# RMSNorm with SiLU on one core: stores move from SyncE's queue to ScalarE's, loads are issued one block earlier

## The chip, the core and the metric

The kernel runs on one core of a Trainium2 chip. Five engines work side by side, each on its own list of instructions, in order: TensorE (PE), VectorE (DVE), ScalarE (ACT), GpSimd (POOL) and SyncE (SP). An instruction waits on semaphores for what it needs, and everything behind it on the same engine waits with it. Transfers between HBM and the on-chip memory are issued by an engine's queue (here SyncE's and ScalarE's) and carried out by 16 DMA engines, which report each finished transfer on a semaphore.

The metric is the time of the whole kernel on the device, in microseconds (us). A profile records one execution; its span runs from the first to the last instruction, and the time of the same execution is a little longer than its span.

## The reference

```python
x = np.random.randn(8, 1024, 2048).astype(np.float32)
gamma = np.random.randn(2048).astype(np.float32)
eps = np.float32(1e-5)

def reference(x, gamma, eps):
    rms = np.sqrt(np.mean(x ** 2, axis=-1, keepdims=True) + eps)
    out = gamma * x / rms
    return (out * (1 / (1 + np.exp(-out)))).astype(np.float32)
```

Each of 8192 rows of 2048 numbers is divided by its root mean square, multiplied by gamma, and passed through SiLU. 64 MiB are read and 64 MiB written.

## The kernel before

The 8192 rows are cut into 16 blocks of 512 rows. A block is one tile `xt` of 128 partitions by 4 rows of 2048 floats (32 KiB in each partition, 4096 KB in all), and it is loaded by one transfer and stored by one transfer. The pool holds six such tiles (`BUFS` = 6, line 33). A load needs a tile that is free, that is, one whose earlier block has been stored.

Before the loop, the row of gamma is fetched by ScalarE's queue (line 93) into one of these six tiles, five blocks are loaded by SyncE's queue (lines 95 and 96, line 51), and TensorE spreads gamma to all partitions by a matrix product with a column of ones (line 99); VectorE copies the result into the tile `g` (line 100).

Then, for each block b, `work(b)` does this:

- The sums of squares of its four rows: two on ScalarE (line 79, Square with accumulation), two on VectorE (line 82).
- `rsqrt` (lines 61 to 72) on VectorE: 15 instructions on 128 x 4 numbers, which give 1/rms by a bit trick and four Newton steps, without ScalarE.
- For each of the four rows, VectorE multiplies by `g` in place (line 87), then ScalarE applies Silu in place with 1/rms as its scale (line 88).
- SyncE stores the tile (line 89). The store waits for the last Silu of the block.

After `work(b)`, SyncE gets the load of block b + LEAD, with LEAD = 5 (lines 103 and 104). It takes the tile of block b - 1, so it waits until the store of block b - 1 has landed. (Block 5 takes the tile in which the row of gamma stood.)

The order is as written: the kernel runs under `manual_schedule`, so each engine gets its instructions in program order, and only semaphores between engines are added. SyncE's list is therefore: loads 0 to 4, store 0, load 5, store 1, load 6, and so on to store 10, load 15, and then stores 11 to 15. A wait of one entry holds all that stand behind it. All these transfers go through one DMA queue. A transfer's semaphore is one of a set of eight that are used again in turn, so a transfer may also have to wait until an older one with the same semaphore has landed.

Of the kernel before, what the change touches and what calls it, by code (L numbers as in the profile page):

```python
# [1 line left out]

# [4 lines left out]

ACT = mybir.ActivationFunctionType
ALU = mybir.AluOpType


@with_exitstack
def kernel(
    ctx: ExitStack,
    tc: tile.TileContext,
    x: bass.AP,
    gamma: bass.AP,
    eps: bass.AP,
    out: bass.AP,
):  # L20

    nc = tc.nc
    P = nc.NUM_PARTITIONS
    f32, i32 = mybir.dt.float32, mybir.dt.int32
    x2 = x.flatten_outer_dims()
    o2 = out.flatten_outer_dims()  # L30
    n, d = x2.shape
    J = 4
    BUFS, LEAD = 6, 5
    nblk = n // (P * J)
    xb = x2.rearrange("(b p j) d -> b p (j d)", p=P, j=J)
    ob = o2.rearrange("(b p j) d -> b p (j d)", p=P, j=J)

    singles = ctx.enter_context(tc.tile_pool(name="singles", bufs=1))
    pool = ctx.enter_context(tc.tile_pool(name="pool", bufs=BUFS))
    small = ctx.enter_context(tc.tile_pool(name="small", bufs=2))  # L40
    psum = ctx.enter_context(tc.tile_pool(name="psum", bufs=1, space=bass.MemoryType.PSUM))

    g = singles.tile([P, d], f32)
    ones = singles.tile([1, P], f32)
    junk_a = psum.tile([P, d], f32, name="junk_a")
    junk_v = psum.tile([P, d], f32, name="junk_v")
    blocks = {}

    def load(b):
        xt = pool.tile([P, J * d], f32, name="xt")  # L50
        nc.sync.dma_start(out=xt, in_=xb[b])
        blocks[b] = xt

    def row(b, j):
        return blocks[b][:, j * d:(j + 1) * d]

    def rsqrt(ss):


        var = small.tile([P, J], f32, name="var")  # L60
        nc.vector.tensor_scalar(out=var, in0=ss, scalar1=1.0 / d, scalar2=float(eps),  # L61
                                op0=ALU.mult, op1=ALU.add)
        y = small.tile([P, J], f32, name="y")
        t = small.tile([P, J], f32, name="t")
        nc.vector.tensor_single_scalar(out=t.bitcast(i32), in_=var.bitcast(i32), scalar=1,  # L65
                                       op=ALU.logical_shift_right)
        nc.vector.tensor_scalar(out=y.bitcast(i32), in0=t.bitcast(i32), scalar1=-1, scalar2=0x5F375A00,  # L67
                                op0=ALU.mult, op1=ALU.add)
        for _ in range(4):
            nc.vector.scalar_tensor_tensor(out=t, in0=y, scalar=-0.5, in1=y, op0=ALU.mult, op1=ALU.mult)  # L70
            nc.vector.tensor_mul(out=t, in0=t, in1=var)  # L71
            nc.vector.scalar_tensor_tensor(out=y, in0=t, scalar=1.5, in1=y, op0=ALU.add, op1=ALU.mult)  # L72
        return y

    def work(b):
        ss = small.tile([P, J], f32, name="ss")
        for j in (0, 2, 1, 3):
            if j < J // 2:
                nc.scalar.activation(out=junk_a, in_=row(b, j), func=ACT.Square,  # L79
                                     accum_out=ss[:, j:j + 1])  # L80
            else:
                nc.vector.tensor_tensor_reduce(  # L82
                    out=junk_v, in0=row(b, j), in1=row(b, j), scale=1.0, scalar=0.0,
                    op0=ALU.mult, op1=ALU.add, accum_out=ss[:, j:j + 1])
        rstd = rsqrt(ss)
        for j in range(J):
            nc.vector.tensor_mul(out=row(b, j), in0=row(b, j), in1=g)  # L87
            nc.scalar.activation(out=row(b, j), in_=row(b, j), func=ACT.Silu, scale=rstd[:, j:j + 1])  # L88
        nc.sync.dma_start(out=ob[b], in_=blocks.pop(b))

    with tc.manual_schedule():
        grow = pool.tile([P, J * d], f32, name="xt")
        nc.scalar.dma_start(out=grow[0:1, 0:d],
                            in_=bass.AP(tensor=gamma.tensor, offset=gamma.offset, ap=[[d, 1], gamma.ap[0]]))
        for b in range(min(LEAD, BUFS - 1)):
            load(b)
        nc.vector.memset(ones, 1.0)  # L97
        for c in range(0, d, 512):
            nc.tensor.matmul(junk_v[:, c:c + 512], ones, grow[0:1, c:c + 512], start=True, stop=True)  # L99
        nc.vector.tensor_copy(out=g, in_=junk_v)  # L100
        for b in range(nblk):
            work(b)
            if b + LEAD < nblk:
                load(b + LEAD)


# [1 line left out]
_INS = ['x', 'gamma', 'eps']  # L108
_OUTS = [((8, 1024, 2048), 'float32')]

_NUMBERS = {'eps': 9.999999747378752e-06}


# [26 lines left out]
```

## Time and profile before

| | |
|---|---|
| Median of three runs | 321.74 us (321.55 to 322.38) |
| The profiled execution | 322.38 us, its span 320.6 us |
| Moved | 67.12 MB read, 67.11 MB written, 419 GB/s over the span |
| Loads, issue to landing | median 30.1 us, shortest 12.3 us |
| Stores, issue to landing | median 38.5 us (30.0 to 46.1) |
| Silu, one row of a block on ScalarE | 2.00 us, 64 of them |
| Multiplication by g, one row on VectorE | 2.28 us, 64 of them |
| Square on VectorE / on ScalarE, one row | 2.30 us / 1.87 us, 32 of each |
| ScalarE idle until line 87 of VectorE | 87.1 us in 62 waits |
| VectorE idle until line 79 of ScalarE | 20.0 us in 15 waits |

The page of a profile gives each engine's busy time and its share of the span; groups of instructions are named by line, engine and operation, `out<-in`. `xt<-in_x_dram` is a load and `out_dram<-xt` a store. "Idle before" is the time in which an engine stood still just before such an instruction, with what ended the wait. In a timeline each row gives the start in us from the span's start, the duration, the engine, the line and the operation; `SPq` and `ACTq` are the queues of SyncE and ScalarE, where an entry is the issuing of a transfer and not the transfer itself. `L121` and `L135` are lines around the kernel, at its start and its end.

### The profile page before, as it was taken

To read this page: it belongs to the slowest core of one execution; us is meant where nothing else is said; L and a number is where in the kernel's file an instruction comes from. 1 tells how busy PE (TensorE), PEld (TensorE's weight loads), DVE (VectorE), ACT (ScalarE), POOL (GpSimd) and SP (SyncE) were. 2 spreads that over 40 slices of the span, in tenths; PEclk is the share of its full clock that TensorE was granted. 3 is DMA by queue.
4 is the path that set the end of the run, shared out by engine and by line. 5 is a ranking of instruction groups with operands and counts; after the bars stand their busy time and mean duration, and the time that the engine had idled before them with its cause. 6 is when DMAs were issued, how large, how long until landed. Compare 5 with 4: busy or idle time off the path is not lost.

```text
span 320.6 us, 656 instructions
## 1 busy us (share of the span) xinstructions
PE 7.2 (2%) x8; PEld 2.5 (1%) x8; DVE 256.7 (80%) x370; ACT 193.1 (60%) x130; POOL 0.2 (0%) x4
## 2 busy tenths in 40 slices
PE   6200000000000000000000000000000000000000
PEld 2000000000000000000000000000000000000000
DVE  0699797989989797979899797979798997979000
ACT  1339486684939395775939393957759393948100
POOL 0000000000000000000000000000000000000000
DMA  8999999999999999999999999999999999999991
GB/s 328 446 405 458 421 429 392 430 417 442 425 425 446 409 450 430 421 437 418 437 446 409 442 429 425 437 429 433 433 414 442 442 421 442 421 433 450 409 446 82
DMA packets 4614, 134.26 MB, mean 419 GB/s; under 512 B 513, under 2 KB 513, under 8 KB 513
## 3 DMA queue, kind: packets, MB, share of 16 engines
q1 hardware_dynamic: 4608, 134.22, 97.8%
q14 instruction: 4, 0.03, 0.0%
q10 hardware_dynamic: 2, 0.01, 0.0%
HBM read 67.12 MB, written 67.11 MB: 419 GB/s over the span
## 4 chain that ended last, share of the span: by engine, by line
DVE 38%; issue 13%; ACT 8%; DVEq 1%
DVE xt L87 30%; ACT junk_a L79 7%; DVE t L70 2%; DVE t L71 2%; DVE y L72 2%; ACT xt L88 1%; DVEq L135 1%; DVE var L61 1%; DVE y L67 1%; DVE t L65 1%
## 5 line engine op out<-in xcount | busy, mean ns | idle before, releaser
L88 ACT ACTIVATE xt<-xt,y 128x2048 f32<-128x2048 f32 x64 | 128.1, 2002 | 92.5 <-DVE xt L87 87.1
L87 DVE TENSOR_TENSOR xt<-xt,g 128x2048 f32<-128x2048 f32 x64 | 142.2, 2283 | 0.0
L82 DVE CUSTOM_DVE_ANT_0 junk_v<-xt 128x2048 f32<-128x2048 f32 x32 | 73.5, 2296 | 1.7 <-DMA xt<-in_x_dram 1.1
L79 ACT ACTIVATE junk_a<-xt 128x2048 f32<-128x2048 f32 x32 | 59.9, 1872 | 11.0 <-DMA xt<-in_x_dram 10.5
L61 DVE TENSOR_SCALAR var<-ss 128x4 f32<-128x4 f32 x16 | 2.7, 170 | 20.1 <-ACT junk_a L79 20.0
L70 DVE SCALAR_TENSOR_TENSOR t<-y 128x4 f32<-128x4 f32 x64 | 10.4, 162 | 2.2
L72 DVE SCALAR_TENSOR_TENSOR y<-t,y 128x4 f32<-128x4 f32 x64 | 10.4, 162 | 2.2
L71 DVE TENSOR_TENSOR t<-t,var 128x4 f32<-128x4 f32 x64 | 10.4, 162 | 2.2
L100 DVE COPY g<-junk_v 128x2048 f32<-128x2048 f32 x1 | 2.3, 2292 | 8.7 <-PE junk_v L99 8.7
L99 PE MATMUL junk_v<-xt,ones 1*128 1x512 f32 x8 | 7.2, 1069 | 2.5 <-DMA xt<-in_gamma_dram 2.5
L79 ACT ACTIVATION_READ_ACCUMULATOR junk_a<-xt 128x1 f32 x32 | 6.0, 186 | 0.0
L82 DVE DVE_READ_ACCUMULATOR2_ANT ss<- 128x1 f32 x32 | 4.5, 140 | 0.0
L67 DVE TENSOR_SCALAR y<-t 128x4 int32<-128x4 int32 x16 | 2.7, 170 | 0.5
L65 DVE TENSOR_SCALAR t<-var 128x4 int32<-128x4 int32 x16 | 2.7, 170 | 0.5
L99 PEld LDWEIGHTS junk_v<-xt,ones 1*128 1x128 f32 x8 | 2.5, 322 | 5.6 <-issue 5.6
L79 ACT ACT_TABLE_LOAD x1 | 1.3, 1283 | 1.3 <-PEq L121 1.3
L88 ACT ACT_TABLE_LOAD x1 | 1.3, 1283 | 0.0
L97 DVE MEMSET ones<- 1x128 f32 x1 | 0.2, 165 | 0.8 <-PEq L121 0.8
L121 POOL MEMSET const-bfloat16-1.0<- 128x1 bf16 x1 | 0.1, 103 | 0.0
L121 POOL MEMSET const-uint8-127<- 128x1 uint8 x1 | 0.1, 103 | 0.0
L121 POOL MEMSET const-float32-1.0<- 128x1 f32 x1 | 0.1, 100 | 0.0
L121 POOL MEMSET const-float32-0.0<- 128x1 f32 x1 | 0.1, 99 | 0.2 <-issue 0.2
## 6 DMA issues: line engine op xcount, KB each, us to landing
xt<-in_x_dram SPq DMA_DIRECT2D x16, 4096.0 KB, 30.1
out_dram<-xt SPq DMA_DIRECT2D x16, 4096.0 KB, 38.5
xt<-in_gamma_dram ACTq DMA_DIRECT2D x1, 8.0 KB
```

Source lines behind the costliest of these rows:

```text
L61: nc.vector.tensor_scalar(out=var, in0=ss, scalar1=1.0 / d, scalar2=float(eps), op0=ALU.mult, op1=ALU.add)
L65: nc.vector.tensor_single_scalar(out=t.bitcast(i32), in_=var.bitcast(i32), scalar=1, op=ALU.logical_shift_right)
L67: nc.vector.tensor_scalar(out=y.bitcast(i32), in0=t.bitcast(i32), scalar1=-1, scalar2=0x5F375A00, op0=ALU.mult, op1=ALU.add)
L70: nc.vector.scalar_tensor_tensor(out=t, in0=y, scalar=-0.5, in1=y, op0=ALU.mult, op1=ALU.mult)
L71: nc.vector.tensor_mul(out=t, in0=t, in1=var)
L72: nc.vector.scalar_tensor_tensor(out=y, in0=t, scalar=1.5, in1=y, op0=ALU.add, op1=ALU.mult)
L79: nc.scalar.activation(out=junk_a, in_=row(b, j), func=ACT.Square, accum_out=ss[:, j:j + 1])
L82: nc.vector.tensor_tensor_reduce(out=junk_v, in0=row(b, j), in1=row(b, j), scale=1.0, scalar=0.0, op0=ALU.mult, op1=ALU.add, accum_out=ss[ ...
L87: nc.vector.tensor_mul(out=row(b, j), in0=row(b, j), in1=g)
L88: nc.scalar.activation(out=row(b, j), in_=row(b, j), func=ACT.Silu, scale=rstd[:, j:j + 1])
L99: nc.tensor.matmul(junk_v[:, c:c + 512], ones, grow[0:1, c:c + 512], start=True, stop=True)
L135: with _tile.TileContext(nc) as tc:
```

## The change

The look-ahead grows from five blocks to six, one more load stands before the loop, and stores are issued by ScalarE's queue.

```diff
-    BUFS, LEAD = 6, 5
+    BUFS, LEAD = 6, 6
...
         for j in range(J):
             nc.vector.tensor_mul(out=row(b, j), in0=row(b, j), in1=g)
             nc.scalar.activation(out=row(b, j), in_=row(b, j), func=ACT.Silu, scale=rstd[:, j:j + 1])
-        nc.sync.dma_start(out=ob[b], in_=blocks.pop(b))
+        nc.scalar.dma_start(out=ob[b], in_=blocks.pop(b))
...
         for b in range(min(LEAD, BUFS - 1)):
             load(b)
...
         nc.vector.tensor_copy(out=g, in_=junk_v)
+        load(BUFS - 1)
         for b in range(nblk):
             work(b)
             if b + LEAD < nblk:
                 load(b + LEAD)
```

SyncE's list is now the 16 loads alone. Load 5 waits for the tile in which the row of gamma stood; load b + 6 takes the tile of block b and waits until store b has landed. ScalarE's list gets 16 stores, each between the last Silu of its block and the Squares of the next. The arithmetic, the tiles and the number and size of the transfers are the same.

## The prediction

> **What bounds the kernel now.** I read the busy shares and DMA queues of the page first, then SyncE's waits, then the timeline of one block and the last stretch.
>
> ```profile
> PE 7.2 (2%) x8; PEld 2.5 (1%) x8; DVE 256.7 (80%) x370; ACT 193.1 (60%) x130; POOL 0.2 (0%) x4
> ...
> q1 hardware_dynamic: 4608, 134.22, 97.8%
> ```
>
> One queue carries every load and store and keeps the 16 DMA engines busy for 97.8% of the span: the kernel is bound by transfers, 32 of 4096 KB. SyncE's own waits say how these are paced:
>
> ```profile
> SPq L51 <- DMA out_dram<-xt: 178.8, 10, 20.1
> SPq L89 <- ACT xt L88: 95.0, 9, 18.8
> SPq L135 <- DMA out_dram<-xt: 21.4, 1, 21.4
> ```
>
> Loads wait for an older store to land (the buffer), in all 178.8 us; 21.4 us pass between the last issue and the last landing. The timeline of SyncE dates the landings, since each of these loads goes out as a store lands:
>
> ```profile
> 62.91 0.33 SPq L51 DMA_DIRECT2D xt<-in_x_dram  x1
> ...
> 82.61 0.33 SPq L51 DMA_DIRECT2D xt<-in_x_dram  x1
> ...
> 102.69 0.33 SPq L51 DMA_DIRECT2D xt<-in_x_dram  x1
> 103.07 0.42 SPq L89 DMA_DIRECT2D out_dram<-xt  x1
> ...
> 242.42 0.33 SPq L51 DMA_DIRECT2D xt<-in_x_dram  x1
> ```
>
> Store 0 (blocks count from 0) landed at 62.91, store 9 at 242.42: nine pairs of a load and a store in 179.5 us, 19.95 us a pair. Between load 0 (its first reader starts at 13.02) and 62.91 lie five transfers, 9.98 each. From 242.42 to the end (the last issue starts at 297.9, its copies land 21.4 later, near 319.7) lie eight, six of them stores: 9.66 each. The stretches of the end:
>
> ```profile
> 298.00:313.00 15.00, 0.00 (x0) 0.00 (x0) 0.00 (x0) 0.00 (x0) 0.00 (x0) 1.00 0.99 426
> 313.00:321.00 8.00, 0.00 (x0) 0.00 (x0) 0.00 (x0) 0.00 (x0) 0.00 (x0) 1.00 0.16 70
> ```
>
> The last two columns are the DMA share and GB/s. All engines are done computing before 298, the transfers run full until 313, and then only 0.16 of the DMA engines still work: some lag some 6 us behind the others, and the slowest sets the end. Compute is second in line, close behind. One block seen on ScalarE and VectorE:
>
> ```profile
> 29.77 2.00 ACT L88 ACTIVATE xt<-xt,y 128x2048 f32<-128x2048 f32 x1 [0.20 <-DVE xt L87]
> 31.68 1.86 ACT L79 ACTIVATE junk_a<-xt 128x2048 f32<-128x2048 f32 x1
> 31.80 0.35 SPq L89 DMA_DIRECT2D out_dram<-xt  x1
> ...
> 35.73 0.17 DVE L61 TENSOR_SCALAR var<-ss 128x4 f32<-128x4 f32 x1 [1.34 <-ACT junk_a L79]
> ```
>
> The last Silu of a block, the two Squares of the next, then VectorE's small steps (which wait 1.34 for the Squares) and its four multiplications, then the last Silu again: a closed chain, 17.73 us a block. It never starves after block 0, so it ends at 31.77 + 15 x 17.73 = 297.8. A block takes 17.73 us of compute and 19.95 of transfers; compute stays ahead because the first five loads run ahead of any store.
>
> **The change, part by part.**
>
> *Removed from SyncE:* 16 stores, 0.33 to 0.42 us each, and with them the order "load k+5 behind store k". That store had to wait for the block's last Silu (95.0 us in all). Worth nothing by itself: the queue was full behind it.
>
> *Load 5 ahead of block 0, the rest one ahead* (LEAD 6). Load 5 now waits only for the gamma row's buffer, which the matmuls free near 9.7, instead of going out at 32.24. The first five loads fill the queue until about 52, so nothing moves sooner: 0 us. Load k+6 waits for store k to land, the same store that frees its buffer now. Sixteen loads, 4096 KB each, stay on SyncE; nothing but loads stands behind a waiting load there.
>
> *Sixteen stores on ScalarE's queue.* Each stands between a block's last Silu and the next block's Squares, and must wait for that Silu to end. Now the Square starts 0.09 before the Silu's end (31.68 against 31.77). Afterwards: 0.09 lost, 0.03 to release (31.77 to 31.80), the issue, and 0.04 to the next instruction (the gamma issue ends at 1.24, the table load after it starts at 1.28). The issue is 0.33 to 0.42 on SyncE and 0.51 for the gamma row on ScalarE. So 0.49 to 0.67, I take 0.58. It lies on the closed chain, 15 times before the last block is done: 7.4 to 10.1, I take 8.7, and compute could end at 306.5 at best. Squares, VectorE's small steps and multiplications all queue behind. The program's order also gives stores 4 to 12 a wait for an older transfer, because they reuse its semaphore: store 5 for load 6, store 11 for load 12, the others for stores three to five blocks older. Those stores landed a block or more before; load 6 lands near 113 against 123 needed, load 12 near 232.5 against 233.2, and the Square behind that store needs load 12 anyway. I cost these waits at 0; if loads slip further, ScalarE stands still with the load, which it would do one instruction later.
>
> *Two rings in place of one.* This decides. From store 0 on, loads and stores no longer take turns of 4 MB in the order of one queue; both wait at the DMA engines all the time. The trace never has two full queues, so the share is bounded: loads first (then nothing starves), stores first (loads fall back until stores run out of computed blocks), and I take one for one, which is what the single queue gives in steady state. The pace of a pair is bounded by 19.32 (twice 9.66, if the stalls of the lagging engines disappear) and something above 19.95. I take 19.95, the row with the same mixture.
>
> Then: store 0 goes out at 31.8, and its bytes move about 1 us later, as load 0's do. At 33.0 the loads done are 1 + (33.0 - 13.0) / 9.98 = 3.0, so 13.0 remain. Now they go one for one with stores: 33.0 + 13.0 x 19.95 = 292.4 for load 15. In the old order it went out at 242.42 behind load 14 and store 10 and landed near 242.4 + 3 x 9.8 = 272. ScalarE would reach its Squares at 280.0 + 8.7 = 288.7: the load is late, load 14 (272.4 against 270.4 needed) slightly so. From landing to the last Silu block 0 shows 13.0 to 31.77, 18.8 us. So block 15 is computed at 292.4 + 18.8 = 311.2. At 292.4 13 stores are done; stores 13 and 14 run until 292.4 + 2 x 9.66 = 311.7, and store 15 follows: 321.4 (from a standstill, by load 0's 12.3, it would be 323.5). I take 321.6. Span 320.6 - 319.7 = 0.9 behind it: 322.5, against 320.6 now, +1.9 us. The profiled execution took 322.38, 0.64 more than the median of the three; the same difference on the median gives 323.6, and with the pace possibly between the two ends I say **323.4 us** (+0.5%).
>
> The Trainium skill speaks against the change: "DMA: Bandwidth & Descriptors", section "Issuing engines are not separate DMA queues", says that transfers started by several engines run on the same 16 DMA engines, interleave, and save no more than the time to issue. No row here shows two full queues. By this rule alone the sum would be the transfers' 319.7 again at best, so no gain, and the cost on ScalarE on top.
>
> **The rivals.**
>
> 1. *The rings cover each other's stalls* (faster). The 6 us that some engines lag may come from changes between loads and stores in one queue; with a second queue such an engine has other work. For it: the 0.16 row, and 9.66 for stores alone against 9.98 mixed. Against: a mixture now occurs at every packet. Price: pace 19.32, load 15 at 33.0 + 13.0 x 19.32 = 284.2, in time; compute sets the end: 306.5, and the last store alone 9.66 to 12.3, I take 11.1: 317.6, span 318.5, -2.1: 319.6 us. It ends on the other side; it decides from a pace under about 19.7.
>
> 2. *Stores get more than half, or mixing slows the engines.* If stores run out of computed blocks, load 15 lands with one store more done, one transfer later: +10 us, 333.4. Each 1% on the pace costs 2.6 us at load 15. For it: the mixture costs 0.3 us a transfer now at its few borders. Against: nothing in the trace shows a slow stretch of mixed work (full shares throughout).
>
> 3. *Loads come first, or nothing moves.* Load 15 lands as early as now, compute ends at 306.5, the slowest DMA engine still ends near 319.7: 321.7 us.
>
> **How the numbers follow.** Forecast 0.42 (322 to 325), rival 1 0.30 (317.5 to 320.5), rival 2 0.18 (326 to 334), rival 3 0.10. Differences under 0.3% (about 1 us, 320.8 to 322.7) can't be told from no change with this kernel. Faster: rival 1 and a little of rival 3, 0.32. Same: the rest of rival 3 and the lower edge of the forecast, 0.17. Slower: 0.51. Range 317.8 to 331: it holds rival 1 down to its short last store and rival 2 up to three quarters of its price.
>
> **What would show it.** Right: 20 us a load and 20 us a store side by side, load 15 landing near 292, ScalarE and VectorE waiting for loads from block 13 on, a ScalarE issue of some 0.4 us and a period of 18.3 us before that, VectorE's wait before line 61 near 1.9. Wrong: load 15 before 288 with the end still set by compute (rival 1), a long VectorE wait for loads in the middle (rival 2), ScalarE held at a store by an older transfer, or an issue that takes ScalarE a microsecond.

## The result, and the profile after

The changed kernel takes 319.48 us (median of 4, 319.35 to 319.61) against 321.64 us (median of 4, 321.17 to 322.38): a ratio of 0.9931, 95% interval 0.9911 to 0.995. It is 0.7% faster where 0.5% slower was forecast; the first rival had 319.6. The profiled execution has a span of 317.6 us, 3.0 less than before; it was the shortest of its four, and that of the kernel before the longest of its four, so this is more than the 2.2 us between the medians.

Busy shares and DMA queues, from the page of the changed kernel:

```profile
PE 7.2 (2%) x8; PEld 2.5 (1%) x8; DVE 256.8 (81%) x370; ACT 194.8 (61%) x130; POOL 0.2 (0%) x4
...
q1 hardware_dynamic: 2304, 67.11, 49.5%
q10 hardware_dynamic: 2306, 67.12, 49.0%
```

Two rings (a ring is the list of packets that one queue has waiting at the DMA engines) now carry half the bytes each. Together they are busy for 98.5% of 317.6, or 312.8 us of an average DMA engine; the one ring had 97.8% of 320.6, or 313.5 (312.7 and 313.7 by the packet records, without the rounding of the shares). So the mean work of an engine fell by only some 1.0 us while the end came 3.0 us earlier: what changed is mostly how far the slowest engine lies behind the mean.

One block border, from the timeline of the changed kernel (start, duration, engine, line, operation):

```profile
29.62 2.00 ACT L88 ACTIVATE xt<-xt,y 128x2048 f32<-128x2048 f32 x1 [0.20 <-DVE xt L87]
31.65 0.38 ACTq L89 DMA_DIRECT2D out_dram<-xt  x1
...
32.07 1.88 ACT L79 ACTIVATE junk_a<-xt 128x2048 f32<-128x2048 f32 x1 [0.45 <-ACT xt L88]
...
36.14 0.17 DVE L61 TENSOR_SCALAR var<-ss 128x4 f32<-128x4 f32 x1 [1.90 <-ACT junk_a L79]
```

The Square starts 0.45 us after the Silu's end, and VectorE waits 1.90 for it instead of 1.34. The issues of later stores lie 18.26 us apart: 0.53 us more a block.

Who waited for whom on the engines, and on SyncE, in the changed kernel:

```profile
DVE var L61 <- ACT junk_a L79: 27.8, 15, 1.9
ACT junk_a L79 <- DMA xt<-in_x_dram: 10.3, 1, 10.3
ACT junk_a L79 <- ACT xt L88: 6.3, 15, 0.5
...
DVE junk_v L82 <- DMA xt<-in_x_dram: 0.8, 1, 0.8
```

```profile
SPq L51 <- DMA out_dram<-xt: 217.3, 10, 45.7
SPq L136 <- DMA out_dram<-xt: 51.3, 3, 29.0
SPq L136 <- DMA xt<-in_x_dram: 33.9, 1, 33.9
```

Compute waits for a load once, at the first block, as before. Nothing starves. The last load is issued at 231.1 (the last start of line 51). After it SyncE stands at the end of the program (line 136) and waits for what is still under way: first for a store that lands at 251.4, then 33.9 for the last load, which lands at 285.3, then for the thirteenth store at 287.7 and 29.0 more for the last one, at 316.7. Load 15 is 7 us earlier than the forecast's 292.4 and close to the rival's 284.2.

The end of the changed kernel, the timeline first and then the same stretches as before (the last two columns are DMA share and GB/s):

```profile
303.57 2.00 ACT L88 ACTIVATE xt<-xt,y 128x2048 f32<-128x2048 f32 x1 [0.20 <-DVE xt L87]
305.61 0.34 ACTq L89 DMA_DIRECT2D out_dram<-xt  x1
```

```profile
298.00:313.00 15.00, 0.00 (x0) 0.00 (x0) 5.54 (x3) 6.98 (x4) 0.00 (x0) 1.00 0.84 360
313.00:321.00 8.00, 0.00 (x0) 0.00 (x0) 0.00 (x0) 0.00 (x0) 0.00 (x0) 1.00 0.31 131
```

Compute ends at 305.6 instead of 297.8. Before it ends most DMA engines have run out of work (a share of 0.54 from 303 to 308), and then all carry the last store, which lands at 316.7.

The packet records of the trace show where the lag went. Nearly every 32 KB packet takes 1.213 us. The excess over that, summed over all 16 engines (packets over by 0.05 us or more):

| Kernel | first 60 us | after 60 us |
|---|---|---|
| before | 25.3 us | 18.0 us |
| changed | 23.5 us | 2.2 us |

Both pay at the start and once more when the first store begins. After that the kernel before loses some 2 us (summed over the engines) in every 20, mostly in the last load packets ahead of a store, most of it on a few of the sixteen engines: five end 3 to 6 us later than most of the others. In the changed kernel this is nearly gone.

### The profile page after: what moved, and what is told of

Same layout as the page of the kernel before. It is cut to its first block, busy times and chain, and to the rows that moved or that the text cites. A ratio compares the mean times of both kernels' runs of the same rounds, so it can differ in the third digit from the quotient of the medians.

```text
span 317.6 us, 637 instructions
## 1 busy us (share of the span) xinstructions
PE 7.2 (2%) x8; PEld 2.5 (1%) x8; DVE 256.8 (81%) x370; ACT 194.8 (61%) x130; POOL 0.2 (0%) x4
## 3 DMA queue, kind: packets, MB, share of 16 engines
q1 hardware_dynamic: 2304, 67.11, 49.5%
## 4 chain that ended last, share of the span: by engine, by line
DVE 58%; ACT 27%; issue 4%; DMA 4%; ACTq 2%; DVEq 1%
DVE xt L87 44%; ACT junk_a L79 17%; ACT xt L88 10%; DMA xt<-in_x_dram 4%; DVE t L70 3%; DVE t L71 3%; DVE y L72 3%; ACTq L89 2%; DVE junk_v L82 1%; DVE t L65 1%; DVE var L61 1%; DVE y L67 1%; DVEq L136 1%; DVE ss L82 0%; DVEq L61 0%
## 5 line engine op out<-in xcount | busy, mean ns | idle before, releaser
L79 ACT ACTIVATE junk_a<-xt 128x2048 f32<-128x2048 f32 x32 | 60.2, 1881 | 17.1 <-DMA xt<-in_x_dram 10.3
L71 DVE TENSOR_TENSOR t<-t,var 128x4 f32<-128x4 f32 x64 | 10.3, 161 | 2.2
```

## The experiments

Several theories were to be told apart on the gain (A: two rings take the stalls out; B: the longer look-ahead; E: the stalls come from contention with compute; G or H: what about a second ring does it), and on what sets the end now (C: compute and the last store; D: the slowest DMA engine; D': that engine is slow because it also fetches instructions; F: it is slow for an unknown reason). A border is a place in a ring where a load is followed by a store.

**The queue alone** (`queue_only`)

```diff
     BUFS, LEAD = 6, 5
...
-        nc.sync.dma_start(out=ob[b], in_=blocks.pop(b))
+        nc.scalar.dma_start(out=ob[b], in_=blocks.pop(b))
```

> The stores on ScalarE's queue, LEAD left at 5, no extra load ahead of the loop. Theory A (two rings take the stalls out of the load-to-store borders; the look-ahead does nothing, since SyncE's list is loads alone either way): the same as the changed kernel, 319.5 us, within 0.3%; span near 317.6, last issue of a store near 305.6. Theory B (the gain is the earlier load 5 and the longer look-ahead): back to 321 to 322 us.

Measured 319.59 us, ratio 0.9947 (0.9928 to 0.9966): theory A. The look-ahead and the early load 5 are worth nothing measurable.

**The look-ahead alone** (`lead_only`)

```diff
-    BUFS, LEAD = 6, 5
+    BUFS, LEAD = 6, 6
...
         nc.sync.dma_start(out=ob[b], in_=blocks.pop(b))
...
+        load(BUFS - 1)
```

> LEAD 6 and load 5 ahead of the loop, the stores left on SyncE's queue. Theory A: no gain; worse, because in SyncE's one list load b+6 now waits for the landing of store b ahead of the issue of store b+1, so that the ring runs empty once a pair; from store 0 on some 1 to 2 us lost a pair, 12 pairs, 335 to 350 us. Theory B: 319 to 320 us.

Measured 354.55 us, ratio 1.1039 (1.1013 to 1.1066): the direction of theory A, and worse than its range. SyncE's queue in the timeline:

```profile
31.80 0.34 SPq L89 DMA_DIRECT2D out_dram<-xt  x1
73.54 0.33 SPq L51 DMA_DIRECT2D xt<-in_x_dram  x1
73.96 0.38 SPq L89 DMA_DIRECT2D out_dram<-xt  x1
96.48 0.33 SPq L51 DMA_DIRECT2D xt<-in_x_dram  x1
96.90 0.38 SPq L89 DMA_DIRECT2D out_dram<-xt  x1
```

Store 1 was ready at 49.5 and goes out at 73.96, behind a load that waits for store 0 to land. Each such landing finds the ring empty, and a pair takes 22.9 us (73.54 to 96.48) instead of 19.95. Idle engines are only half of the loss. The page of this run has the mean engine busy for 93.3% of its span of 353.8 us:

```profile
q1 hardware_dynamic: 4608, 134.22, 93.3%
```

That is 330 us of work against 313.7 in the kernel before, for the same bytes: half of the 33 us by which the span grew are slow packets. By the packet records a pair has some 28 us of excess over the 16 engines: some 11 in the first packets after the empty ring (0.7 us an engine) and some 15.5 where the load turns to the store (1.0 us an engine). The two halves of the change belong together: a look-ahead as long as the pool is only affordable when stores don't stand behind the loads.

**The store behind the next block's Squares** (`late_store`)

```diff
+    def finish(b):
+        nc.scalar.dma_start(out=ob[b], in_=blocks.pop(b))
+        if b + LEAD < nblk:
+            load(b + LEAD)
...
+        if b > 0:
+            finish(b - 1)
         rstd = rsqrt(ss)
...
-        nc.scalar.dma_start(out=ob[b], in_=blocks.pop(b))
...
-            if b + LEAD < nblk:
-                load(b + LEAD)
+        finish(nblk - 1)
```

> The changed kernel with each store issued on ScalarE after the two Squares of the next block (the last one after the last Silu), where ScalarE waits for VectorE anyway. Both theories of the end: the 0.53 us a block on ScalarE go, the period falls from 18.26 to 17.73 and the last store is issued near 298 instead of 305.6. Theory C (compute and the last store set the end): 2 to 4 us faster than the changed kernel, 315.5 to 317.5 us. Theory D (the slowest DMA engine, never idle, sets the end at 316.3 of the span): the same as the changed kernel, 319 to 319.8 us.

Measured 319.08 us, ratio 0.9929 (0.9913 to 0.9946), 0.4 us less than the changed kernel (and 0.5 less than `queue_only`, measured beside it): theory D. The 0.53 us a block did go from ScalarE (VectorE waits 1.34 again), but compute now waits 7.8 us for loads on VectorE and the last store leaves at 301.3. Its last stretches:

```profile
308.00:313.00 5.00, 0.00 (x0) 0.00 (x0) 0.00 (x0) 0.00 (x0) 0.00 (x0) 1.00 0.97 419
313.00:318.00 5.00, 0.00 (x0) 0.00 (x0) 0.00 (x0) 0.00 (x0) 0.00 (x0) 1.00 0.03 13
```

A share of 0.03 over 5 us of 16 engines is 2.4 us of one engine: fifteen are done by 313.7, and one alone works until 316.0. In the changed kernel the packets of the last store, which waits for compute, end at 316.2 to 316.4, and one engine that never stands idle before that store carries its last packet until 316.3. Two limits lie on top of each other, and removing one shows the other.

**The last store in four pieces** (`split_last`)

```diff
+            if b == nblk - 1:
+                nc.scalar.dma_start(out=ob[b][:, j * d:(j + 1) * d], in_=row(b, j))
+        if b < nblk - 1:
             nc.scalar.dma_start(out=ob[b], in_=blocks.pop(b))
```

> The changed kernel with the last block stored in four pieces of one row each, each issued behind its Silu. Theory C: the transfer left behind the last Silu shrinks from 4096 to 1024 KB, the DMA engines' idle time near 302 goes: 1.5 to 3 us faster than the changed kernel, 316.5 to 318 us. Theory D: within 0.3% of the changed kernel, 319 to 319.8 us.

Measured 319.27 us, ratio 0.9937 (0.992 to 0.9954): 0.2 us under the changed kernel where theory C had 1.5 to 3: theory D again.

**A copy on one ring, and on two** (`copy_one_ring`, `copy_two_rings`): the kernel before and the changed kernel without their compute.

> The kernel before with all of work(b) left out but the store: x is copied to the output by the same 32 transfers in the same order on SyncE's one ring. Theory A (the border from a load to a store in one ring costs some engines 0.2 to 0.8 us, whatever the compute engines do): the same slow packets near the last load packet before each store, the slowest engine some 4 to 6 us behind the fast ones, 318 to 322 us. Theory E (the stalls come from compute engines reading and writing the tiles beside the transfers): the stalls go, 314 to 316 us.

> The changed kernel with all of work(b) left out but the store: the same copy, stores on ScalarE's ring. Theory A: no slow packets after the first store's start, all engines end within 1 us of each other, 313.5 to 316 us; 4 to 6 us less than the copy on one ring. Theory E: the same as the copy on one ring.

Measured 320.41 us (median of 10, 319.12 to 321.58) on one ring and 316.83 us (median of 4, 316.58 to 318.96) on two; against the kernel before on the same chip 0.997 (0.9954 to 0.9986) and 0.9854 (0.9818 to 0.989). The rings alone are worth 3.6 us by the medians, with no compute beside them: theory A holds in the main, and E falls as the only cause. The excess after 60 us is 9.0 us on one ring and 2.1 us on two. Three things limit this. The gain is a little under the 4 to 6 us expected. The profiled executions took 319.12 us on one ring and 318.96 us on two, so the traces show the difference in the slow packets and not in their spans: on two rings one engine still ended 2.2 us behind the others. And on one ring the slow packets begin only at 120 us and add up to half of the 18.0 us in the kernel before; whether compute adds the other half, or single executions differ by as much, isn't shown.

**Twice the borders in one ring** (`halves_in_turn`, and `halves_in_pairs` to compare with)

```diff
-        nc.sync.dma_start(out=xt, in_=xb[b])
...
+        return [(xt[:, c:c + H], xb[b][:, c:c + H]) for c in (0, H)]
...
-            work(b)
-            if b + LEAD < nblk:
-                load(b + LEAD)
+            s = work(b)
+            l = load(b + LEAD) if b + LEAD < nblk else []
+            issue([p for two in zip(s, l) for p in two] if l else s)
```

> The kernel before with each transfer cut into two of 2048 KB (two rows of each partition), and SyncE's list in the loop: half a store, half a load, half a store, half a load. Twice as many borders from load to store in one ring. Theory A: the lag of the slowest engine doubles, 4 to 8 us over the next kernel's time. Otherwise: the same time as the next.

> The same halves, listed as two halves of the store, then two halves of the load: as many borders as the kernel before. All theories: 320 to 324 us, if the smaller transfers and their more frequent semaphores cost nothing; it is what the kernel before it is compared with.

Measured 322.15 us in turn and 323.30 us in pairs (ratios 1.0013, 1.0001 to 1.0025, and 1.0043, 1.0024 to 1.0062). The kernel with twice as many borders is not slower but 0.4% faster, and both lose the same after 60 us (8.6 and 8.4 us, in packets half as long). So the loss is not a fixed price for each border: that part of theory A fell.

**Two rings, each with both directions** (`copy_mixed_rings`)

```diff
+    def ring(b):
+        return nc.scalar if b % 2 else nc.sync
...
-        nc.sync.dma_start(out=xt, in_=xb[b])
+        ring(b).dma_start(out=xt, in_=xb[b])
...
-        nc.sync.dma_start(out=ob[b], in_=blocks.pop(b))
+        ring(b).dma_start(out=ob[b], in_=blocks.pop(b))
```

> The copy without compute (all of work(b) left out but the store), both loads and stores of even blocks on SyncE's ring and of odd blocks on ScalarE's: two rings, but each with borders from loads to stores in it. Theory G (any second ring with work takes up the stalls): as the copy with loads and stores on rings of their own, 316.5 to 317.5 us. Theory H (a ring must hold one direction only; a border inside a ring costs the same with a second ring beside it): as the copy on one ring, 319.5 to 321.5 us. A ring stands empty for about 2 us after each of its stores lands; with both rings empty at once it would be slower than either, and tell nothing.

Measured 327.51 us, ratio 1.0206 (1.0166 to 1.0245), slower than either copy. The two rings fell into step: SyncE issues its loads at 79.2, 118.3 and 159.9, ScalarE at 81.6, 121.9 and 162.5. After 60 us the excess is 98 us, in bursts 40 us apart in which the engines lose 0.8 to 1.6 us each, much as all do at the first store of every kernel. So a second ring is not enough by itself, and theory G as stated falls. H is not proved by it, since in step the rings make every engine turn at the same time; what two mixed rings out of step would do, no run shows.

**Fewer instructions to fetch** (`two_steps`, on the kernel with the late store)

```diff
-        for _ in range(4):
+        for _ in range(2):
```

> The kernel with the store behind the Squares, and two Newton steps in place of four: 96 of VectorE's 395 instructions fewer, and 1.2 us of compute a block less. Theory D' (the slowest DMA engine sets the end, and it is slow because it fetches instructions in packets of 8 KB between the data; three of VectorE's four fetches seen stand on one engine, each with a gap of 0.3 us and a data packet some 0.5 us too long): one fetch fewer, 0.6 to 1 us faster than with four steps (319.1), 318.0 to 318.6. Theory F (it is slow for another reason): the same, 318.8 to 319.4.

Measured 317.89 us (317.84 to 318.24), ratio 0.989 (0.9875 to 0.9905). The instruction queue in the pages of the changed kernel (the kernel with the late store has the same line), of this one, and of the next but one:

```profile
q14 instruction: 4, 0.03, 0.0%
```

```profile
q14 instruction: 3, 0.02, 0.0%
```

```profile
q14 instruction: 7, 0.06, 0.0%
```

The columns are packets, MB and share. Each of these packets brings 8 KB of instructions through one of the same 16 DMA engines: 0.31 us on it, and in most cases the data packet behind it is 0.24 to 0.58 us too long. In the kernel with four steps three of the four stand, by the timing of the packets, on the engine that ends last; with two steps one fetch is gone, and the end comes 1.2 us earlier, a little more than theory D' had. The fetches and the slow packets behind them add up to 2.4 us with four steps and 1.7 with two, so they make 0.7 of the 1.2 us; slow packets of 0.43 us at 76.8 and 0.11 at 118.3, which this execution doesn't have, make up the rest, and the first is far from any fetch. The compute that is saved can hardly be what helps, since VectorE waits 30.9 us for loads here (7.8 with four steps); that it is in part the fetch fits the records and one run, and no second run confirms it. The two kernels ran on different chips, on both of which the kernel before took 321.58.

**With the last store in pieces** (`two_steps_split`)

```diff
+            if b == nblk - 1:
+                nc.scalar.dma_start(out=ob[b][:, j * d:(j + 1) * d], in_=row(b, j))
...
-        finish(nblk - 1)
```

> The same with the last block stored in four pieces, each behind its Silu. The end stays with the slowest DMA engine: within 0.5 us of the kernel with two steps, 317.6 to 318.6; and faster than both the kernel before and the changed one.

Measured 318.48 us, ratio 0.9906 (0.989 to 0.9921): 0.6 us slower than without the pieces. The single last store is not the limit, and in pieces it is more work: its packets of 8 KB take 0.309 us, 1.236 for 32 KB in place of 1.213, some 0.2 us an engine. The other 0.4 us are not explained.

**More instructions on an idle engine** (`pool_fill`)

```diff
+        fill = singles.tile([P, 1], f32)
+        for _ in range(400):
+            nc.gpsimd.memset(fill, 0.0)
```

> The changed kernel with 400 fills of a number per partition added on the idle GpSimd (its own instructions, 25 KB of them, three more fetches in the first 50 us). Theory D': if they come from the DMA engine that already fetches VectorE's, 1.5 to 2.6 us slower than the changed kernel, 321 to 322; if from another, that one falls behind by as much and the end moves by 0 to 0.5 us. Theory F: the same as the changed kernel, 319.5, and no new slow packets.

Measured 319.98 us, ratio 0.9952 (0.9937 to 0.9967), 0.5 us over the changed kernel. Three more fetches, two of them, by the timing of the packets, on the engine that serves VectorE, but 1.5 to 2.6 us did not follow. No engine went without a pause before the last store, and that one stood idle for 1.0 us, so it was not the limit; ScalarE's wait for load 0 grew from 10.3 to 10.8, the start of compute with it, and the end with that. The price that D' put on a fetch is not borne out here, at least for fetches in the first 50 us.

The fastest kernel of the study is `two_steps`: stores on ScalarE's ring, issued behind the next Squares, and two Newton steps. It is 1.1% faster than the kernel before, and the copy without compute, at 316.83, is only 1.1 us below it.

## Why the prediction was wrong

**The step that failed** is the pace of the two rings: "I take 19.95, the row with the same mixture". The pair took (285.3 - 33.0) / 13.0 = 19.4 us, next to the lower bound of 19.32; over 13 pairs this is the 7 us by which load 15 came early. The row had the same mixture of bytes, but it dates landings, and a landing follows the slowest engine (its last packet ends at 319.38 in the kernel before, the last landing is at 319.75). So the 19.95 holds the growing lag of that engine. By the bytes moved, the kernel before was hardly slower (the kernel before first, the changed one second; GB/s in the last column):

```profile
62.00:242.00 180.00, 0.00 (x0) 0.00 (x0) 161.50 (x232) 121.45 (x82) 0.00 (x0) 1.00 1.00 430
62.00:242.00 180.00, 0.00 (x0) 0.00 (x0) 156.26 (x229) 117.89 (x79) 0.00 (x0) 1.00 1.00 433
```

The 8.39 MB of a pair take 19.5 us at 430 GB/s and 19.4 at 433. What the second ring took away is the lag: in one ring a few engines lost time at the borders, 18.0 us of excess after 60 us, and with a ring for each direction hardly any does (2.2). The bound was right, the rival that used it had 319.6, and the choice between the ends was wrong. The medians of the two copies show the gain without compute.

**What followed from it.** With load 15 at 285.3 no block is late, against "the load is late" in the forecast, and compute rather than the load leads to the last store.

**One for one** held: between 33 and 286 us 13.0 loads land, and the thirteenth store lands at 287.7. The Trainium skill, "DMA: Bandwidth & Descriptors", section "Queues, rings and completion order", says that a DMA engine takes its rings in turn, packet by packet; the landings agree with it. The section "Issuing engines are not separate DMA queues", weighed in the prediction, promises nothing from a second issuing engine beyond the time to issue. Here the measurement decides otherwise: 3.6 us of 320 in the copy. That isn't issue time: an issue takes 0.33 to 0.43 us, and the DMA engines are full meanwhile (a share of 1.00 from 62 to 298 us in both copies).

**ScalarE's 0.58 us a block** measured 0.53: the issue took 0.34 to 0.38, near SyncE's, not the 0.51 of the gamma row. Compute ended at 305.6 (306.5 "at best" in the forecast). The waits for older transfers by their semaphore cost nothing, as costed. VectorE's wait of 1.9 was right.

**Nothing for the look-ahead** was right; the queue alone gives the whole gain.

**The last store and the tail.** 11.1 us for the last store was rival 1's figure and is what it took (305.6 to 316.7), with 0.9 behind it. Yet rival 1 is right on the time and only half right on the cause. It had compute set the end; with 15 x 0.53, some 8 us, taken off ScalarE's chain, the last store left 4.3 us earlier and the kernel ended 0.4 us earlier, because one DMA engine has work without a pause until 316.3 in the changed kernel, as late as the last store. The forecast and the rivals compared limits as if one of them must be alone.

**Rivals 2 and 3.** Mixing slows nothing (433 GB/s from 62 to 242 us against 430 before, and packets of 1.213 us in both), and stores did not get ahead. Nor did loads come first: load 15 landed at 285.3, not near the 272 of the old order.

**What stays open** is why a border in one ring costs an engine anything. It can't be the change of direction alone: with two rings a load lands only every 19.4 us, though its eight packets on an engine take 9.7, so each engine goes back and forth between loads and stores within every transfer, and loses almost nothing. Nor is it a fixed price a border; it falls mostly on engines that are already late, and it costs every engine 0.8 to 1.6 us when all turn at once (1.0 in `lead_only`). That is a description of the records and not a mechanism.

## What to carry to other kernels

When one ring carries large loads and stores by turns and the transfers are the bound, try a ring for each direction: here 1.1% without compute, 0.7% with it. Before a pace taken from landings goes into a sum, compare it with the bytes moved in the same stretch: here 19.95 and 19.5 us a pair. Look at how far the slowest DMA engine lies behind the mean, since a mean share of 97.8% hid 6 us of lag. Before paying for a shorter compute chain, test whether a second limit lies right behind the first: issue the store later, or cut it, and see whether the end moves.

## What the hardware showed besides

Instructions arrive through the same 16 DMA engines as the data, 8 KB at a time: four fetches of 0.31 us in the kernel, three of them some 90 us apart (56.6, 148.7 and 242.8 us), which fits VectorE's list. So, when the transfers are the bound, the instructions of an engine that is nowhere near the bound may have a price: with 96 fewer on VectorE one fetch went and the kernel took 1.2 us less, of which fetches account for some 0.7; three more fetches on GpSimd's account did not cost what this would say. And 4 MB transfers on two rings that both change direction can lock in step: that copy took 327.5 us, 2% more than the copy on one ring.
